# One more 2 MiB slot in the weight ring of a decoder layer with 32 experts, and the expert activation computed inside its own PSUM bank

## The chip, the cores and the metric

The kernel runs on one core of one Trainium2 chip. The metric is the device time of one execution in microseconds (us), from three timed runs. Times inside the execution come from one profiled run, whose span is the time from its first to its last instruction.

## The reference, cut to what matters

One decoder layer over 256 tokens of width 1024, all in float32. A token mixer (input projection, a spatial gate, attention, two branch products, an output product) is followed by LayerNorm and a routed FFN with 32 experts, of which every token takes 4:

```python
logits = x @ w_router + b_router                 # 256 x 32
top_val, top_idx = lax.top_k(logits, 4)
gate = softmax(top_val)
for every expert e, over the tokens that picked it:
    gu  = xe @ w_up[e] + b_up[e]                 # 1024 x 2048 weights, 8 MiB
    g   = minimum(gu[:, :F], 7.0)
    u   = clip(gu[:, F:], -7.0, 7.0)
    act = (u + 1.0) * (g * sigmoid(1.702 * g))
    y   = act @ w_down[e] + b_down[e]            # 1024 x 1024 weights, 4 MiB
out = layer_norm(alpha * h + sum of gate * y)
```

All 32 experts are used, so 32 times 12 MiB of weights are read from HBM once.

## The kernel before

**Two stages.** Stage 1 (to about 270 us of the span) is the mixer: 20 pieces of weights, split into two float32r parts and multiplied. Stage 2 is the routed FFN. In between stands the router: logits, top 4, the counts of each expert, and a sorting of the experts by their number of tokens, after which the kernel knows which expert is taken at which position p = 0 ... 31. Positions 0 and 3 always hold experts 0 and 1, so their weights can be loaded before the router has run; the other 30 expert numbers (`ids`) come out of it.

**Blocks.** A position has room for 1, 2 or 3 blocks of 32 tokens (15, 14 and 3 positions, 52 blocks in all). For each block, TensorE does `up_bias` (L696, L697: the bias rows start a PSUM bank), `up_quad` (L703: 64 instructions, four column tiles of 32 side by side), then `swiglu` runs on other engines, `act_T` transposes the activation (L720), `spread` transposes the weighted one-hot matrix (L685), `down_half` is the down product (L730: 64 instructions), `y_of` copies it out (L737) and `scatter` adds it to the output (L745). `gather` (L662) picks the tokens of a group of up to 4 blocks.

**The order on TensorE** is written out by hand (`steps`): `a` is the first half of a position's up weights, `b` the second half, `d` the down weights. The usual order is ... `b(p-1)`, `a(p)`, `d(p-1)`, `b(p)`, `a(p+1)` ..., so the bias matmuls of the next position come right after the last up product of the one before; ahead of a position with three blocks a `d` step lies in between. Small work (`act_T`, `spread`, `gather`, `scatter`) is put in between by a counter (`later`, `tick`). The order on the other engines is the framework's.

**PSUM.** The up product of a block takes one of two `mm` banks in turn (a third block of a position takes the `at` bank), all transposes share one `tp` bank. The next owner of an `mm` bank waits until `swiglu` has read it for the last time.

**`swiglu` before** (L709 to L713): VectorE clips the gate half into SBUF, ScalarE takes the sigmoid, VectorE clips the linear half into SBUF (its last read of the bank), GpSimd multiplies gate and sigmoid, VectorE forms the activation.

**The weight ring** has 10 half slots of 2 MiB, as five tiles `R0` to `R4`. Four of them are also the buffers of stage 1. `order` lists the halves in the order of loading. `free(p, k)` is called when TensorE's last product with a half has been issued; it calls `load_next`, which starts the next load into that slot on SP's DMA queue. For positions 5 to 29 (`WHOLE`) two halves are loaded with one 4 MiB DMA, when both slots of a tile are free. Ten halves can be loaded ahead of the router: both experts known beforehand, without the down weights of position 3. The eleventh load in `order` needs `ids` (L190 reads a register from it).

Of the kernel before, what the change touches and what calls it, by code (L numbers as in the profile page):

```python
# [54 lines left out]
def tile_kernel(ctx: ExitStack, tc: tile.TileContext, x, ln_in_g, ln_in_b, w_in, gmlp_ln_g, gmlp_ln_b,  # L55
# [25 lines left out]
    R = [ringp.tile([P, 8192], FT, name=f"R{i}") for i in range(4)]  # L81
# [84 lines left out]
    heads = [(0, "a"), (0, "b"), (0, "d"), (3, "a"), (3, "b")]  # L166
    order = [(p, k + h) for p, k in heads + [u for u in uses if u not in heads] for h in "01"]
# [4 lines left out]
    def half(slot):  # L172
        return R[slot // 2][:, slot % 2 * 4096:slot % 2 * 4096 + 4096]

    done = []

    def load_next(slot):
# [4 lines left out]
        n = 2 if p in WHOLE else 1  # L182
# [10 lines left out]
        if n == 2:  # L193
            assert h == 0 and slots[0] % 2 == 0 and slots[1] == slots[0] + 1
            to = R[slots[0] // 2]
        else:
            to = half(slot)
# [97 lines left out]
    def constants():  # L295
# [13 lines left out]
        k["rows"] = keep.tile([P, P], FT, name="rows_of")  # L309
        nc.gpsimd.iota(k["rows"].rearrange("p (n s) -> p n s", n=4), pattern=[[-1, 4], [0, CAP]], base=0,  # L310
                       channel_multiplier=1, **iota)
        nc.vector.tensor_scalar(rows0, k["rows"], 0.0, None, op0=OP.is_equal)
# [5 lines left out]
        k["onesf"] = keep.tile([2 * NE, P], FT, name="onesf")  # L318
# [247 lines left out]
    for i in range(n_pieces):  # L566
# [69 lines left out]
    R.append(sp2.tile([P, 8192], FT, name="R4"))  # L636
    load_next(8)
    load_next(9)
# [3 lines left out]
    low, up = 0, 64  # L642
    tables = sp2.tile([P, D + T * P], FT, name="tables")
    gT = tables[:NE + 1, :T * P].rearrange("p (t q) -> p t q", t=T)
    rkT = tables[:NE, T * P:2 * T * P].rearrange("p (t q) -> p t q", t=T)
    bd = tables[up:up + NE + 1, :D]
    gD = tables[up:up + NE + 1, D:].rearrange("p (t q) -> p t q", t=T)

    gates = sp2.tile([P, T, NE + 1], FT, name="gates")
# [24 lines left out]
    def weighted(rank, gate, k):  # L674
        ptg = sp2.tile([P, T, P], FT, name="ptg", bufs=2)
        for t in range(T):
            nc.vector.tensor_scalar(ptg[:, t].rearrange("p (n s) -> p n s", n=4),
                                    iota_s[:, None, k * CAP:(k + 1) * CAP].to_broadcast([P, 4, CAP]), rank(t), gate(t),
                                    op0=OP.is_equal, op1=OP.mult)
        return ptg  # L680

    def spread(ptg):
        ps = ps_tp()
        for t in range(T):
            nc.tensor.transpose(ps[:, t * P:(t + 1) * P], ptg[:, t], ident)  # L685
        qt = sp2.tile([P, T, P], FT, name="qt", bufs=4)
        nc.vector.tensor_copy(qt, ps[:, :T * P].rearrange("p (t q) -> p t q", t=T))
        return qt

    def bias_rows(e4):  # L690
        at = sp2.tile([P, P], FR, name="rows", bufs=2)
        nc.vector.tensor_scalar(at, const["rows"], e4, None, op0=OP.is_equal)
        return at
# [40 lines left out]

    def y_of(py):
        y = sp2.tile([P, 256], FT, name="y", bufs=3)
# [10 lines left out]


# [7 lines left out]
    keys = sp2.tile([NE, NE], FT, name="keys")  # L756
# [88 lines left out]
    def spread_row(at, j):  # L845
        ps = ps_tp()
        nc.tensor.matmul(ps, const["onesf"][at:at + 1], tables[at:at + 1, j * 512:(j + 1) * 512], start=True, stop=True)
# [3 lines left out]
    def residual(j):  # L851
        ps = spread_row(0, j)

        def part(t, todo):
            ys = []
            for i in range(2):
                y = sp2.tile([P, 256], FT, name="y", bufs=3)
                z = zn[:, t].rearrange("p (c q) -> p q c", c=NC)[:, 64 * j + 32 * i:64 * j + 32 * i + 32]
                nc.vector.scalar_tensor_tensor(y.rearrange("p (q c) -> p q c", c=NC), z, ALPHA,
                                               ps[:, i * 256:(i + 1) * 256].rearrange("p (q c) -> p q c", c=NC),  # L860
# [3 lines left out]
            def add():  # L864
                for i in range(2):
                    n = 2 * j + i
                    to = yacc[j][:, i, t * 256:(t + 1) * 256]
                    nc.tensor.matmul(to, gD[:, t], bd[:, n * 256:(n + 1) * 256], start=False, stop=False)
# [28 lines left out]
    def masks(g):  # L897
        pts[g] = sp2.tile([P, T, GRP * CAP], FT, name="pt", bufs=2)
# [110 lines left out]
    def logits(t, ps):  # L1009
# [3 lines left out]
        lt = sp2.tile([P, T, P], FT, name="ptg", bufs=2)[:, 0]  # L1013
# [3 lines left out]
    def pick(t, ps):  # L1017
        lg = sp2.tile([P, NE], FT, name="lg", bufs=2)
        nc.vector.tensor_tensor(lg, ps[:, P:P + NE], rb, op=OP.add)
        v8 = sp2.tile([P, 8], FT, name="v8", bufs=2)  # L1020
        nc.vector.max(v8, lg)
        i8 = sp2.tile([P, 8], U32, name="i8", bufs=2)
        nc.vector.max_index(i8, v8, lg)
        i4 = sp2.tile([P, TOPK], FT, name="i4", bufs=2)
        nc.vector.tensor_copy(i4, i8[:, :TOPK])
        eq = sp2.tile([P, NE, TOPK], FT, name="eq", bufs=1)
# [16 lines left out]
    nc.sync.dma_start(bd[:NE], b_down[0])  # L1043
    nc.sync.dma_start(bd[NE:], ln_mix_b)
# [17 lines left out]
    for t in range(T):  # L1062
        lg, v8 = picks[t]
        nv = sp2.tile([P, 4], FT, name="nv", bufs=2)
        nc.vector.tensor_scalar(nv[:, 0:1], v8[:, 0:1], -1.0, None, op0=OP.mult)
        ex = sp2.tile([P, NE], FT, name="ex", bufs=1)
# [13 lines left out]
    with tc.manual_schedule(engines=MS):  # L1080
        def free(p, k):
            load_next(ring[p, k])
# [14 lines left out]
        for kind, p in steps[1:-1]:  # L1097
# [3 lines left out]
            if kind == "b":  # L1101
# [8 lines left out]
                if p == LEFT_AT + 1:  # L1110
                    load_row(0, ln_mix_g)
                    load_row(32, ln_ffn_g)
                if p in RESIDUAL_AT:
                    later(1, lambda p=p: residual(RESIDUAL_AT.index(p)))
                if p == NORM_AT:
                    load_row(0, ln_ffn_b)
                if p == NE - 2:
                    gb = R[ring[p, "b0"] // 2][:, :2 * D].rearrange("p (a d) -> p a d", a=2)
# [46 lines left out]

    with tc.For_i(0, n_left) as i:
# [6 lines left out]
        ra, rbb, rd, rt = [R[ring[k] // 2] for k in ((NE - 1, "a0"), (NE - 1, "b0"), (NE - 2, "d0"), (NE - 1, "d0"))]  # L1173
        nc.sync.dma_start(ra, up_e[:, 0:8192])
        nc.sync.dma_start(rbb, up_e[:, 8192:16384])
        nc.sync.dma_start(rd.rearrange("p (h n) -> p h n", h=2), wd[bass.ds(e, 1)].rearrange("o p h n -> (o p) h n"))
        four = sp2.tile([P, 1], FT, name="four")
        nc.vector.tensor_scalar(four, cur[:, 2 * T], 4.0, None, op0=OP.mult)
        pt = sp2.tile([P, T, GRP * CAP], FT, name="pt", bufs=2)
# [54 lines left out]
```

## Time and profile before

| | |
|---|---|
| median of 3 runs | 1202.85 us (1202.83 to 1206.37) |
| profiled execution, its own time | 1203.3 us |
| its span | 1201.5 us |
| mean granted TensorE clock | 0.957 of full speed |
| busy shares: TensorE, VectorE, ScalarE, GpSimd | 92%, 35%, 18%, 9% |
| moved by DMA | 451.06 MB, 448.58 MB of it read from HBM |

The profiled execution's own time is 1.8 us longer than its span (work around the first and last instruction), and 0.45 us above the median. A DMA share of 1.00 means that all 16 DMA engines were busy for the whole stretch. TensorE's busy time counts pipelined matmuls and is no measure of a full array.

### The profile page before, as it was taken

How to read it: one execution, taken by the hardware profiler on the slowest of the kernel's cores; microseconds unless marked ns; L12 is line 12 of the kernel's file. 1: busy time of each engine (PE TensorE's matmuls, PEld its weight loads, DVE VectorE, ACT ScalarE, POOL GpSimd, SP SyncE). 2: the span in 40 equal slices, each digit the busy share in tenths (PEclk: the TensorE clock that was granted, in tenths of full speed). 3: DMA queues.
4: the chain of work that ended last, by engine and by line, in shares of the span. 5: the costliest groups of instructions: out<-in, count | busy, mean ns of one | idle time of the engine just before them, and what ended most of it. 6: DMA issues, size and time to landing. Idle time of an engine off the chain costs nothing.

```text
span 1201.5 us, 21808 instructions
## 1 busy us (share of the span) xinstructions
PE 1106.8 (92%) x9725; PEld 576.6 (48%) x9725; DVE 416.8 (35%) x779; ACT 216.2 (18%) x359; POOL 110.8 (9%) x121
## 2 busy tenths in 40 slices
PE   8999999999999889889999989999999899999794
PEld 6778788874544244343434343434333424343231
DVE  7964645554413122214132231411323223121203
ACT  5445643422201001000001010100010101010010
POOL 3800200000100000001010000000100010000000
PEclk8999999999999879889999999899999999999788
DMA  9554557667999999999999999999999999999993
GB/s 358 190 210 143 215 203 288 253 247 292 408 430 430 431 430 430 436 433 425 429 435 430 431 431 432 431 429 432 434 429 428 435 428 431 431 434 429 428 426 152
DMA packets 44208, 451.06 MB, mean 375 GB/s; under 512 B 2968, under 2 KB 3628, under 8 KB 26064
## 3 DMA queue, kind: packets, MB, share of 16 engines
q1 hardware_dynamic: 43504, 449.47, 89.3%
q8 instruction: 78, 1.28, 0.4%
q10 hardware_dynamic: 608, 0.16, 0.1%
q14 instruction: 18, 0.15, 0.0%
HBM read 448.58 MB, written 1.05 MB: 374 GB/s over the span
## 4 chain that ended last, share of the span: by engine, by line
PE 72%; DMA 21%; DVE 4%; ACT 1%; POOL 1%; issue 1%; ACTq 0%; DVEq 0%; SPq 0%; POOLq 0%
PE mm L703 20%; PE mm L530 18%; PE at L730 15%; DMA R<-in_w_down_dram 15%; DMA R<-in_w_up_dram 6%; PE tp L662 5%; PE ac L745 4%; PE tp L720 2%; PE tp L685 1%; PE mm L696 1%; POOL gg L712 1%; DVE gg L709 1%; PE at L703 1%; DVE wlo L480 1%; PE mm L697 0%
## 5 line engine op out<-in xcount | busy, mean ns | idle before, releaser
L703 PE MATMUL mm<-R,hT 128*32 128x512 f32 x3136 | 378.7, 609 | 12.7 <-DMA R<-in_w_up_dram 12.7
L730 PE MATMUL at<-R,actT 128*32 128x256 f32 x3328 | 220.4, 405 | 21.8 <-DMA R<-in_w_down_dram 14.8
L703 PEld LDWEIGHTS mm<-R,hT 128*32 128x32 f32 x3136 | 89.2, 111 | 194.1 <-issue 171.9
L709 DVE TENSOR_SCALAR gg<-mm 64x512 f32<-64x512 f32 x49 | 33.5, 683 | 360.4 <-PE mm L703 360.0
L730 PEld LDWEIGHTS at<-R,actT 128*32 128x32 f32 x3328 | 101.0, 115 | 115.2 <-issue 30.8
L712 POOL TENSOR_TENSOR gg<-gg,sg 64x512 f32<-64x512 f32 x52 | 66.4, 1277 | 837.8 <-ACT sg L710 837.8
L480 DVE TENSOR_TENSOR wlo<-R,whi 128x1024 fp32r<-128x1024 f32 x80 | 112.4, 1416 | 76.1 <-ACT whi L472 75.6
L530 PE MATMUL mm<-whi,hTh 128*128 128x512 f32 x256 | 100.6, 401 | 0.8 <-ACT R L489 0.8
L530 PE MATMUL mm<-wlo,hTh 128*128 128x512 f32 x256 | 100.0, 398 | 0.5 <-DVE wlo L480 0.5
L472 ACT ACTIVATE whi<-R 128x1024 fp32r<-128x1024 f32 x80 | 84.4, 1057 | 86.7 <-PE mm L530 81.5
L530 PE MATMUL mm<-whi,hTl 128*128 128x512 f32 x256 | 99.9, 398 | 0.0
L710 ACT ACTIVATE sg<-gg 64x512 f32<-64x512 f32 x52 | 32.8, 630 | 304.5 <-DVE gg L709 282.4
L737 ACT ACTIVATE y<-at 128x256 f32<-128x256 f32 x52 | 20.0, 384 | 333.6 <-PE at L730 333.6
L662 PEld LDWEIGHTS tp<-pt,xn 128*128 128x128 f32 x448 | 56.1, 197 | 28.7 <-DVE hT L667 17.9
L662 PE MATMUL tp<-pt,xn 128*128 128x128 f32 (+2 forms) x448 | 65.9, 291 | 0.0
L745 PE MATMUL ac<-y,qt 32*128 32x256 f32 x832 | 59.9, 402 | 0.5 <-ACT y L737 0.5
L745 PEld LDWEIGHTS ac<-y,qt 32*128 32x128 f32 x832 | 37.9, 185 | 37.8 <-issue 35.6
L670 ACT ACTIVATE hT<-tp,lm 128x128 f32<-128x128 f32 (+2 forms) x58 | 25.6, 445 | 165.8 <-PE tp L662 165.7
L530 PEld LDWEIGHTS mm<-wlo,hTh 128*128 128x128 f32 x256 | 48.0, 188 | 13.4 <-DVE wlo L480 2.3
L722 DVE COPY actT<-tp 128x256 f32<-128x256 f32 x52 | 22.1, 425 | 93.2 <-PE tp L720 93.1
L720 PEld LDWEIGHTS tp<-ident,act 64*128 64x128 f32 x208 | 28.8, 209 | 53.1 <-issue 19.5
L530 PEld LDWEIGHTS mm<-whi,hTh 128*128 128x128 f32 x256 | 48.0, 188 | 12.0 <-ACT R L489 0.9
(273 smaller groups left out, 843.7 us busy)
## 6 DMA issues: line engine op xcount, KB each, us to landing
R<-in_w_up_dram SPq DMA_DIRECT2D x50, 4096.0 KB, 34.8
R<-in_w_down_dram SPq DMA_DIRECT2D x25, 4096.0 KB, 37.2
R<-in_w_up_dram SPq DMA_DIRECT2D x28, 2048.0 KB, 12.0
R<-in_w_in_dram SPq DMA_DIRECT2D x13, 2048.0 KB, 8.7
R<-in_w_down_dram SPq DMA_DIRECT2D x13, 2048.0 KB, 33.2
R<-in_w_branch_a_dram SPq DMA_DIRECT2D x2, 2048.0 KB
R<-in_w_branch_b_dram SPq DMA_DIRECT2D x2, 2048.0 KB, 8.3
R<-in_w_out_dram SPq DMA_DIRECT2D x2, 2048.0 KB
```

The source lines that it names most:

```text
L472: nc.scalar.activation(hi, w, AF.Copy)
L480: nc.vector.tensor_tensor(lo, w, hi.bitcast(FT), op=OP.subtract)
L530: nc.tensor.matmul(ps[t], (a_l if k == 1 else a_h)[:, c, t * P:(t + 1) * P], (lo if k == 2 else hi)[:, cc], start=c == 0 and k == 0, stop= ...
L662: nc.tensor.matmul(ps[:, i * w:(i + 1) * w], zn[:, t, c * P:(c + 1) * P], pt[:, t, :w], start=t == 0, stop=t == T - 1)
L670: nc.scalar.activation(dst[:, c, :w], ps[:, i * w:(i + 1) * w], AF.Identity, scale=lm[:, 0, c:c + 1], bias=lm[:, 1, c:c + 1])
L703: nc.tensor.matmul(ps[n * CAP:(n + 1) * CAP], xs[:, c], w[:, o:o + 512], start=False, stop=c == NC - 1)
L709: nc.vector.tensor_scalar(gg, ps[:2 * CAP], LIMIT, None, op0=OP.min)
L710: nc.scalar.activation(sg, gg, AF.Sigmoid, scale=SW_ALPHA)
L712: nc.gpsimd.tensor_tensor(gg, gg, sg, op=OP.mult)
L720: nc.tensor.transpose(ps[:, c * 2 * CAP:(c + 1) * 2 * CAP], v[:, c], ident[:2 * CAP, :2 * CAP])
L730: nc.tensor.matmul(py[n * CAP:(n + 1) * CAP, :256], at[:, c, h], w[:, o:o + 256], start=h == 0 and c == 0, stop=h == 1 and c == 3)
L745: nc.tensor.matmul(to[n // 2][:, n % 2, t * 256:(t + 1) * 256], qt[s, t], y[s], start=start and t == 0, stop=stop and t == T - 1)
```

## The change

The ring gets an eleventh half slot, so the first half of position 3's down weights can also be loaded before the router. Slots 0 to 7 are now one tile, and slots 8 to 10 another. A 4 MiB load may take any two neighbouring free slots that are freed one after the other; otherwise each half is loaded by itself. Counted through the program, 75 loads of 4 MiB and 42 of 2 MiB become 61 and 70.

The room for the slot comes from smaller tables: the bias `b_down` is loaded in two halves of columns, one-hot matrices are stored once instead of four times, `onesf` is one column that is broadcast, router temporaries live in the activation buffers, and the mask buffer `pt` has one copy instead of two. Three consequences are instructions: `spread` uses eight 32-column matmuls instead of two transposes, `residual` builds its row of gains from `lm` with eight broadcast matmuls instead of loading and spreading a row, and `swiglu` works in place: sigmoid and clipped linear half are written back into the block's own PSUM bank, and VectorE does the product that GpSimd did.

```diff
-    R = [ringp.tile([P, 8192], FT, name=f"R{i}") for i in range(4)]
+    pieces = [ringp.tile([P, 8 * 4096], FT, name="R")]
+    R = [pieces[0][:, i * 8192:(i + 1) * 8192] for i in (2, 0, 1, 3)]
...
-    heads = [(0, "a"), (0, "b"), (0, "d"), (3, "a"), (3, "b")]
-    order = [(p, k + h) for p, k in heads + [u for u in uses if u not in heads] for h in "01"]
+    heads = [(0, "a"), (0, "b"), (3, "a"), (3, "b"), (0, "d")]
+    order = [(p, k + h) for p, k in heads for h in "01"] + [(3, "d0")]
+    order += [(p, k + h) for p, k in uses for h in "01" if (p, k + h) not in order]
...
-    def load_next(slot):
+    def load_next(slot, behind=None):
...
-        n = 2 if p in WHOLE else 1
+        n = 2 if p in WHOLE and k[1] == "0" and done[0] != 7 and done[0] + 1 in (done[1:] or [behind]) else 1
...
-            for slot in (4, 5, 6, 7):
+            for slot in (2, 3, 6, 7):
                 load_next(slot)
...
-            for slot in ((2, 3), (0,), (1,))[i - n_pieces + 3]:
+            for slot in ((0, 1), (4,), (5,))[i - n_pieces + 3]:
...
-    R.append(sp2.tile([P, 8192], FT, name="R4"))
-    load_next(8)
-    load_next(9)
+    pieces.append(sp2.tile([P, 3 * 4096], FT, name="R8"))
+    for slot in (9, 10, 8):
+        load_next(slot)
...
     def weighted(rank, gate, k):
-        ptg = sp2.tile([P, T, P], FT, name="ptg", bufs=2)
+        ptg = sp2.tile([P, T, CAP], FT, name="ptg", bufs=2)
...
     def spread(ptg):
         ps = ps_tp()
         for t in range(T):
-            nc.tensor.transpose(ps[:, t * P:(t + 1) * P], ptg[:, t], ident)
+            for n in range(4):
+                nc.tensor.matmul(ps[n * CAP:(n + 1) * CAP, t * P:(t + 1) * P], ptg[:, t], ident, start=True, stop=True)
...
     def swiglu(ps):
-        act = sp2.tile([2 * CAP, 512], FT, name="act", bufs=3)
-        gg = sp2.tile([2 * CAP, 512], FT, name="gg", bufs=2)
-        sg = sp2.tile([2 * CAP, 512], FT, name="sg", bufs=1)
-        nc.vector.tensor_scalar(gg, ps[:2 * CAP], LIMIT, None, op0=OP.min)
-        nc.scalar.activation(sg, gg, AF.Sigmoid, scale=SW_ALPHA)
-        nc.vector.tensor_scalar(act, ps[2 * CAP:], LIMIT, -LIMIT, op0=OP.min, op1=OP.max)
-        nc.gpsimd.tensor_tensor(gg, gg, sg, op=OP.mult)
-        nc.vector.scalar_tensor_tensor(act, act, 1.0, gg, op0=OP.add, op1=OP.mult)
-        return act
+        if not act_bufs:
+            tile_ = sp2.tile([P, 512], FT, name="act", bufs=2)
+            act_bufs.extend((tile_, o) for o in (0, 2 * CAP))
+        tile_, o = act_bufs.pop(0)
+        act = tile_[o:o + 2 * CAP]
+        gate, lin = ps[:2 * CAP], ps[2 * CAP:]
+        nc.vector.tensor_scalar(act, gate, LIMIT, None, op0=OP.min)
+        nc.scalar.activation(gate, act, AF.Sigmoid, scale=SW_ALPHA)
+        nc.vector.tensor_scalar(lin, lin, LIMIT, -LIMIT, op0=OP.min, op1=OP.max)
+        nc.vector.tensor_tensor(act, act, gate, op=OP.mult)
+        nc.vector.scalar_tensor_tensor(act, lin, 1.0, act, op0=OP.add, op1=OP.mult)
+        return act, o
...
     def residual(j):
-        ps = spread_row(0, j)
+        ps = ps_tp()
+        for c in range(NC):
+            nc.tensor.matmul(ps[:, c * 64:(c + 1) * 64], lm[:, 0, c:c + 1].to_broadcast([P, P]),
+                             ident[:, 64 * j:64 * j + 64], start=True, stop=True)
...
-        pts[g] = sp2.tile([P, T, GRP * CAP], FT, name="pt", bufs=2)
+        pts[g] = sp2.tile([P, T, GRP * CAP], FT, name="pt", bufs=1)
...
+        freed = [(p, k + h) for p, k in uses for h in "01"]
+
         def free(p, k):
-            load_next(ring[p, k])
+            i = freed.index((p, k)) + 1
+            load_next(ring[p, k], ring[freed[i]] if i < len(freed) else None)
```

## Rows read from the trace of the kernel before

**Rows 1.** The profile page, part 2: DMA rate in 40 slices of 30 us.

```profile
GB/s 358 190 210 143 215 203 288 253 247 292 408 430 430 431 430 430 436 433 425 429 435 430 431 431 432 431 429 432 434 429 428 435 428 431 431 434 429 428 426 152
```

**Rows 2.** Windows: busy us of each engine, granted clock, DMA share, GB/s.

```profile
280.00:285.00 5.00, 4.94 (x44) 2.77 (x46) 3.26 (x22) 2.10 (x4) 0.00 (x0) 1.00 0.01 2
285.00:290.00 5.00, 5.00 (x48) 2.63 (x44) 3.31 (x18) 1.45 (x4) 0.00 (x0) 1.00 0.53 184
...
763.00:1187.00 424.00, 384.13 (x4006) 164.88 (x4006) 97.12 (x218) 37.67 (x78) 29.59 (x24) 0.95 0.99 423
330.00:1170.00 840.00, 770.55 (x7814) 330.90 (x7810) 207.12 (x473) 72.79 (x149) 61.04 (x48) 0.95 1.00 431
```

**Rows 3.** Timeline of SP's queue, 267 to 291 us: start, length, DMAs issued.

```profile
267.73 0.81 SPq L212 DMA_DIRECT2D R<-in_w_up_dram  x2
...
286.49 0.38 SPq L212 DMA_DIRECT2D R<-in_w_up_dram  x1
```

**Rows 4.** What SP's queue waited for, 262 to 290 us: total, times, longest.

```profile
SPq L190 <- DVE nv L1065: 15.6, 1, 15.6
```

**Rows 5.** Loads into the ring issued from 585 to 615 us: issue to landing.

```profile
DMA to landing us min/median/max: 23.1/23.1/23.1
```

**Rows 6.** The chain that ended last, after 1100 us: start, length, what.

```profile
1161.50 24.53 DMA R<-in_w_down_dram
```

**Rows 7.** What TensorE waited for, 330 to 1187 us: total, times, longest.

```profile
PE at L730 <- DMA R<-in_w_down_dram: 14.8, 11, 2.5
PE mm L696 <- DVE act L711: 13.8, 10, 2.0
PE mm L703 <- DMA R<-in_w_up_dram: 12.7, 3, 6.1
PE tp L720 <- DVE act L713: 10.7, 3, 3.6
```

**Rows 8.** The same, 763 to 1187 us.

```profile
PE at L730 <- DMA R<-in_w_down_dram: 10.8, 9, 2.5
...
PE mm L703 <- DMA R<-in_w_up_dram: 7.8, 2, 6.1
```

**Rows 9.** Timeline of VectorE around the end of position 11 (two blocks).

```profile
602.70 0.68 DVE L709 TENSOR_SCALAR gg<-mm 64x512 f32<-64x512 f32 x1 [17.78 <-PE mm L703]
603.41 0.69 DVE L711 TENSOR_SCALAR act<-mm 64x512 f32<-64x512 f32 x1
```

**Rows 10.** Timeline of TensorE: bias matmuls of positions 12 and 13.

```profile
604.28 0.50 PE L696 MATMUL mm<-bup_h,rows 128*128 128x512 f32 x1
...
627.11 0.47 PE L696 MATMUL mm<-bup_h,rows 128*128 128x512 f32 x1 [0.96 <-DVE act L711]
```

**Rows 11.** Groups of instructions: busy us, mean ns, idle before.

```profile
L712 POOL TENSOR_TENSOR gg<-gg,sg 64x512 f32<-64x512 f32 x52 | 66.4, 1277 | 837.8 <-ACT sg L710 837.8
L710 ACT ACTIVATE sg<-gg 64x512 f32<-64x512 f32 x52 | 32.8, 630 | 304.5 <-DVE gg L709 282.4 <-POOL gg L712 22.1
L503 DVE TENSOR_TENSOR R<-mm,R 128x512 f32<-128x512 f32 x4 | 2.8, 692 | 0.0
L847 PE MATMUL tp<-tables,onesf 1*128 1x512 f32 x12 | 10.3, 952 | 2.3 <-ACT R L879 2.3
L345 PE MATMUL mm<-wr,lm 128*128 128x32 f32 x16 | 3.0, 356 | 2.4 <-DMA wr<-in_w_router_dram 2.4
```

**Rows 12.** Timeline of TensorE: transposes between up products, and the router's 32-column product.

```profile
275.29 0.65 PE L1012 MATMUL ac<-hT,wr 128*32 128x128 f32 x16
...
312.70 0.44 PE L685 MATMUL tp<-ident,ptg 128*128 128x128 f32 x2
313.07 1.06 PE L703 MATMUL mm<-R,hT 128*32 128x512 f32 x8
```

**Rows 13.** Windows after two of the four 2.0 us waits at L696.

```profile
662.00:666.00 4.00, 4.00 (x34) 1.53 (x38) 0.88 (x2) 0.00 (x0) 0.40 (x1) 1.00 1.11 479
810.00:814.00 4.00, 4.00 (x22) 1.01 (x24) 0.88 (x2) 0.00 (x0) 0.01 (x1) 0.57 1.11 475
```

More of the change, by code (lines that the diff above doesn't have):

```diff
@@ L172, in half @@
     def half(slot):
[L173 removed]
+        return pieces[slot // 8][:, slot % 8 * 4096:slot % 8 * 4096 + 4096]
     done = []
[L177 removed]
+    def load_next(slot, behind=None):
         done.append(slot)
@@ L193, in load_next @@
         if n == 2:
-            assert h == 0 and slots[0] % 2 == 0 and slots[1] == slots[0] + 1
-            to = R[slots[0] // 2]
+            lo = slots[0] % 8 * 4096
+            assert h == 0 and slots[1] == slots[0] + 1
+            to = pieces[slots[0] // 8][:, lo:lo + 8192]
         else:
@@ L307, in constants @@
         nc.gpsimd.iota(k["iota_p"], pattern=[[0, 1]], base=0, channel_multiplier=1, **iota)
[L309 to L312, printed above, removed]
+        k["rows"] = keep.tile([P, 4], FT, name="rows_of")
+        nc.gpsimd.iota(k["rows"], pattern=[[-1, 4]], base=0, channel_multiplier=1, **iota)
+        nc.vector.tensor_scalar(rows0.rearrange("p (n s) -> p n s", n=4),
+                                k["rows"][:, :, None].to_broadcast([P, 4, CAP]), 0.0, None, op0=OP.is_equal)
         k["stack"] = keep.tile([P, NE], FT, name="stack")
@@ L746, in scatter @@
                                  start=start and t == 0, stop=stop and t == T - 1)
+    y_bufs = [sp2.tile([P, 256], FT, name=f"y{i}") for i in range(2)] + [wr.rearrange("p c e -> p (c e)")]
     tab = sp2.tile([P, 2 * T + 1, NB], FT, name="tab")
@@ L755, in tile_kernel @@
     nb = sp2.tile([NE, 1], BF, name="nb")
-    keys = sp2.tile([NE, NE], FT, name="keys")
+    keys = scratch[:NE, 480:512]
     perm = sp2.tile([NE, NB], FT, name="perm")
@@ L828, in place_table @@
             if lo >= NE:
-                nc.tensor.matmul(ps[:, t * n:(t + 1) * n], const["onesf"][:NE], shift, start=False, stop=True)
+                nc.tensor.matmul(ps[:, t * n:(t + 1) * n], const["onesf"][:NE].to_broadcast([NE, P]), shift, start=False, stop=True)
             nc.tensor.matmul(ps[:, (T + t) * n:(T + t + 1) * n], gT[:NE, t], cols, start=True, stop=True)
@@ L1116, in tile_kernel @@
                     load_row(0, ln_ffn_b)
+                    load_row(32, ln_ffn_g)
                 if p == NE - 2:
-                    gb = R[ring[p, "b0"] // 2][:, :2 * D].rearrange("p (a d) -> p a d", a=2)
+                    gb = half(ring[p, "b0"])[:, :2 * D].rearrange("p (a d) -> p a d", a=2)
                     for a in range(2):
@@ L1163, in tile_kernel @@
         close()
+    kept = (ring[NE - 2, "b0"], ring[NE - 1, "a0"])
+    spare = [half(slot) for slot in range(11) if slot not in kept]
+    w_e, rt = spare[:6], spare[6]
     with tc.For_i(0, n_left) as i:
@@ L1172, in tile_kernel @@
         up_e = wu[bass.ds(e, 1)].rearrange("o p n -> (o p) n")
[L1173 to L1176, printed above, removed]
+        down_e = wd[bass.ds(e, 1)].rearrange("o p h n -> (o p) h n")
+        for h in range(4):
+            nc.sync.dma_start(w_e[h], up_e[:, h * 4096:(h + 1) * 4096])
+        for h in range(2):
+            nc.sync.dma_start(w_e[4 + h], down_e[:, h])
         four = sp2.tile([P, 1], FT, name="four")
         nc.vector.tensor_scalar(four, cur[:, 2 * T], 4.0, None, op0=OP.mult)
-        pt = sp2.tile([P, T, GRP * CAP], FT, name="pt", bufs=2)
+        pt = sp2.tile([P, T, GRP * CAP], FT, name="pt", bufs=1)
         for t in range(T):
```

80 lines of the change are left out of this document (45 added, 35 removed).

## The prediction

> **What bounds the kernel now.** I read the slices first: the DMA rate is uneven in the first ten slices, 408 GB/s in the eleventh, and then 425 to 436 until the last [rows 1]. Over 330 to 1170 us the 16 DMA engines are busy for the whole time, at 431 GB/s [rows 2]. So the second stage ends when the weights have been read; what matters is how much of them has been read before the steady stretch, and whether anything opens a hole in it.
>
> The one hole near its start is at 280 us: the share is 0.01 in one window of 5 us and 0.53 in the next [rows 2], 4.95 + 2.35 = 7.3 us without transfers. SP's queue shows why: at 267.7 us it issues the last two of the ten loads that need no `ids`, and the eleventh goes out at 286.5 us [rows 3], after 15.6 us of waiting for `ids` [rows 4]. The ring is full and the next expert is not known.
>
> Then the depth of the queue. A 4 MiB load takes 4.19 MB / 431 GB/s = 9.7 us alone. The slowest stretch for TensorE has 23.1 us from issue to landing [rows 5], so at least 13 us of other loads lie ahead of each new one, and TensorE may come that much later before the DMA engines run dry. At the end, the last quarter of the last load lands at 1161.5 + 24.5 = 1186.0 us [rows 6]; from there to the end of the span are 15.5 us of product, scatter, LayerNorm and output that the change leaves alone.
>
> TensorE is a close second. From 330 to 1187 us it waits 14.8 + 12.7 = 27.5 us for weights, 13.8 us for an `mm` bank and 10.7 us for the activation [rows 7], and its granted clock is 0.95 on average [rows 2]: 857 us times 0.05 is 43 us of full-speed work lost at the lower level.
>
> **The change part by part.**
>
> *Eleventh slot.* One more half, 2.097 MB, is loaded before `ids` is there. At 431 GB/s that is 4.9 us, and it fits into the 7.3 us hole. Order and releases of the loads that follow (experts 1 and 2) are unchanged, so the steady stretch starts as before with 2.097 MB less to read: **-4.9 us**. It can't be more by much, since the stretch has no other hole, and it is 0 if the slot is not free before 286.5 us. The slot is cut from the buffers of stage 1, whose last products end at the time of the two issues at 267.7 us [rows 3]; I take the full amount.
>
> *61 and 70 loads instead of 75 and 42.* 14 more issues on SP's queue. With 13 us or more of loads queued [rows 5] they hide; without that cover each would cost a fraction of a microsecond. 0.
>
> *`swiglu` in the bank.* Before, the bank is free when the linear half has been clipped: 602.70 to 603.41 + 0.69 = 604.10 us [rows 9], and the bias matmul of position 12 starts at 604.28 us without a wait [rows 10]. Now the bank is held to the end of the last VectorE operation: clip 0.68, sigmoid 0.63 [rows 11], product and final operation at 0.69 each (the nearest row is the product with one PSUM input, L503 [rows 11]), with about 0.15 us of hand-overs: free at about 602.70 + 2.85 = 605.55, its owner starts at 605.7 us. TensorE waits **1.4 us** where it waited 0. Behind the bias matmul in TensorE's queue stands all of the next position.
>
> How often: I went through all bias matmuls in the timeline. 13 positions follow a two-block position directly and take its first bank (604.28 is one), 0 to 1.4 us. 6 two-block positions follow a one-block position, and their second block takes its bank; there the wait of 0.96 us [rows 10] becomes 2.4. In 4 places a two-block position follows another, and the second bank was waited for 2.0 us already; that grows by about 0.4 us, because TensorE comes 1.4 us later. The 0.96 and 2.0 us waits make up the 13.8 us [rows 7]. Sum: 19 x 1.4 + 4 x 0.4 = **28 us more of TensorE**. If VectorE takes up the next block's clip in between, 0.7 us more in 17 of these places, 40 us; the lower end is 0 for those whose waits fall before data that isn't there yet.
>
> The three places where the transposes wait directly for the activation (3.6 us each [rows 7]) gain: GpSimd's 1.28 us becomes VectorE's 0.69 [rows 11], -0.6 each, **-2 us**. VectorE gets 52 x 0.69 = 36 us more over 900 us at 35% busy: hidden, but for the waits counted.
>
> *`spread`.* Two transposes take 313.07 - 312.70 = 0.37 us of TensorE's time; the same form as the new one, 16 instructions of 32 columns, takes 0.65 us with its run-out [rows 12]. Between 0 and +0.28 us; I take 0.1 since most of the difference is run-out, for 48 blocks **+5 us**, at most 13.
>
> *`residual`.* A spread row takes two instructions of 0.95 us, that overlap; eight broadcast products are 16 instructions, as in L345 with 3.0 us [rows 11]. +1 to +2 us twice: **+3 us**. Its loads fall away. `pt` with one copy, scratch in the activation buffers: masks are written after the gather of the group before has run, so I see no new wait; if there is one it is like that of a bank.
>
> **Does TensorE keep up?** More work: 28 - 2 + 5 + 3 = **34 us**. Cover: 27.5 us of waiting for weights [rows 7], which shrinks as TensorE gets later, and the share of the lost clock that follows from those waits. Half of 43 us is my choice, 21 us (some drops follow other waits). From 48 us the 4.9 us go off, by which the weights now come earlier: 43 us. 34 is less than 43. Late in the span the same sum is 9 x 1.4 + 1 + 24 x 0.1 - 1 = 15 us against 10.8 + 7.8 = 18.6 us [rows 8] plus 424 x 0.05 / 2 = 11, less 4.9: 25 us. So the end is still that of the DMA stream, by a margin of about 10 us. In between TensorE falls further behind, but the 13 us of queue [rows 5] and the new slot's 4.9 hold the DMA engines full.
>
> The forecast is made against the profiled execution: 1203.3 - 4.9 = **1198.4 us**; against the median of 1202.85, 0.45 lower, it would be 1198.0.
>
> **The rivals.**
>
> *TensorE uses up the cover (no change).* If hand-overs are longer or VectorE interleaves, the extra work is 34 + 12 to 16 us, and 3 to 7 us beyond the cover, and so much later than the shifted stream: 1201 to 1206 us. For it speaks that the margin is thin; against it that most waits fall in the middle, where waits for weights come after them.
>
> *The clock (slower).* A wait for a bank can end in the lower clock. After the four 2.0 us waits the windows show 1.00 twice and 0.57 or 0.60 twice (one of each [rows 13]); after the 0.96 us waits it stays at 1.00. At 0.57, four microseconds lose 1.7 us. If the six waits of 2.4 us and half of the 13 new ones end so, it is 12 x 1.7 = 20 us on top of 34: 54 against 43, and the end comes 11 us after the shifted stream, at 1198.4 + 11 = **1209 us**, up to 1215 with the interleaving. It decides from about 8 us beyond the cover, that is with 10 such drops. The Trainium skill, "TensorE: Matmul & The Clock Gate", section "A second HAM failure mode: psum-queue depth-cycling", describes this: PSUM banks cycled through make TensorE idle briefly between groups of matmuls so often that its clock goes up and down. By that rule all 19 waits would cost a drop; the trace agrees for half of the 2.0 us waits and for none of the 0.96 us ones.
>
> *The slot brings nothing.* If slot 8, 9 or 10 waits for a buffer of the mixer's end, its load goes out with the eleventh, and time stays at 1202 to 1204 us. Against it: the two loads of before went out right at the end of the last product [rows 3].
>
> **How the numbers follow.** About 0.3%, 3.6 us, is what a measurement of this kernel can tell from no change. Forecast 0.5 (faster), TensorE using up the cover 0.25 and a slot without effect 0.05 (same, 0.3 together), the clock 0.2 (slower). The range starts at 1196 us (the 4.9 us, and 22 / 430 of 30 us, 1.5 us, if the new slot also fills the slice with 408 GB/s [rows 1]) and reaches to the clock rival's 1209 us; above lie its worst cases, about 0.15.
>
> **What would show it.** Right: no window near 280 us with an empty DMA, a twelfth load at 286 us, 431 GB/s up to a last landing 5 us earlier, L696 waiting some 40 us in all, waits for weights cut by half or more. Wrong: the last `b` and `d` steps start well after their weights have landed, or windows under 0.95 of the clock after bank waits, or a DMA rate under 425 GB/s in the steady stretch.

## The result and the profile after

The changed kernel takes 1243.11 us (median of 4 runs, 1240.68 to 1245.65), the kernel before 1204.37 us in the same comparison: a ratio of 1.0321, with a 95% interval of 1.0306 to 1.0337. The forecast was 1198.4 us and a range up to 1209. The profiled execution took 1241.12 us, with a span of 1239.4.

The page: DMA rate in 40 slices, and the shares of the chain that ended last by engine.

```profile
GB/s 341 191 204 180 225 170 325 186 330 356 425 428 433 428 423 426 434 431 424 424 430 428 395 420 382 425 385 377 420 423 407 379 424 409 388 393 423 428 404 37
...
PE 83%; DVE 12%; ACT 3%; issue 1%; DMA 0%; ACTq 0%; POOL 0%; DVEq 0%
```

The rate is full up to the 22nd slice. In 7 of the 17 slices from there to the last but one it is below 400, where [rows 1] have 425 to 436. The chain holds no DMA: before, its last links were loads [rows 6], and now TensorE, with VectorE, sets the end.

Windows around the hole at 280 us, and of the two long stretches. The last two lines are from the end of the ramp to TensorE's last weight product, first of the changed kernel, then of the kernel before.

```profile
280.00:285.00 5.00, 4.94 (x41) 2.83 (x43) 3.26 (x21) 2.09 (x3) 0.00 (x0) 1.00 0.91 385
285.00:290.00 5.00, 5.00 (x48) 2.67 (x44) 3.38 (x21) 1.45 (x4) 0.00 (x0) 1.00 0.48 156
330.00:1170.00 840.00, 744.67 (x8174) 334.23 (x8168) 223.59 (x508) 66.81 (x142) 0.00 (x0) 0.95 0.98 414
763.00:1187.00 424.00, 376.44 (x4250) 167.88 (x4242) 116.44 (x259) 34.72 (x73) 0.00 (x0) 0.96 0.96 406
330.00:1226.00 896.00, 792.97 (x8714) 355.04 (x8708) 237.08 (x533) 72.37 (x152) 0.00 (x0) 0.95 0.96 406
```

```profile
330.00:1188.00 858.00, 784.16 (x7998) 337.37 (x7994) 210.45 (x479) 74.19 (x152) 62.30 (x49) 0.95 1.00 426
```

The first window of the hole is filled: a share of 0.91 where [rows 2] have 0.01. The second has 0.48, so about 3 us of the 7.3 are left empty. But from 330 us on TensorE needs 896 us instead of 858, 38 us more, which is the whole loss. Of these, 792.97 - 784.16 = 8.8 us are more busy time and 103.0 - 73.8 = 29.2 us more idle time. The mean clock is 0.95 in both.

SP's queue: start, length, loads issued; and its wait for `ids`.

```profile
268.00 1.28 SPq L217 DMA_DIRECT2D R<-in_w_down_dram  x3
...
286.75 10.51 SPq L217 DMA_DIRECT2D R<-in_w_up_dram  x3
...
SPq L194 <- DVE act L1096: 14.8, 1, 14.8
```

Three loads go out at 268 us where two did [rows 3]: the eleventh slot is free in time and takes its load ahead of `ids`.

What TensorE waited for, 330 to 1230 us: total, times, longest.

```profile
PE mm L712 <- DVE act L733: 67.1, 26, 3.3
PE tp L742 <- DVE act L733: 11.1, 4, 3.6
```

The wait for a bank is 67.1 us where [rows 7] have 13.8 and the prediction some 42, 54 at most. The waits for weights, 27.5 us in [rows 7], are gone from the list of this window: in it, the weights are there before TensorE.

Timelines around the end of position 11 (VectorE, ScalarE, TensorE), then one later place with a single block (VectorE, TensorE) and a `spread` behind it. In brackets: idle time before the instruction, and what ended it.

```profile
609.78 0.68 DVE L729 TENSOR_SCALAR act<-mm 64x512 f32<-64x512 f32 x1 [17.78 <-PE mm L719]
611.12 0.71 DVE L731 TENSOR_SCALAR mm<-mm 64x512 f32<-64x512 f32 x1 [0.66 <-ACT mm L730]
611.86 0.68 DVE L729 TENSOR_SCALAR act<-mm 64x512 f32<-64x512 f32 x1
612.58 0.68 DVE L732 TENSOR_TENSOR act<-act,mm 64x512 f32<-64x512 f32 x1
613.29 0.71 DVE L731 TENSOR_SCALAR mm<-mm 64x512 f32<-64x512 f32 x1
613.90 0.69 DVE L733 SCALAR_TENSOR_TENSOR act<-mm,act 64x512 f32<-64x512 f32 x1
...
610.50 0.59 ACT L730 ACTIVATE mm<-act 64x512 f32<-64x512 f32 x1 [6.64 <-DVE act L729]
...
614.74 0.77 PE L712 MATMUL mm<-bup_h,rows 128*128 128x512 f32 x1 [3.31 <-DVE act L733]
615.30 0.63 PE L713 MATMUL mm<-bup_l,rows 128*128 128x512 f32 x1
615.86 5.26 PE L719 MATMUL mm<-R,hT 128*32 128x512 f32 x24
...
639.32 0.68 DVE L729 TENSOR_SCALAR act<-mm 64x512 f32<-64x512 f32 x1 [12.70 <-PE mm L719]
...
642.12 0.69 DVE L733 SCALAR_TENSOR_TENSOR act<-mm,act 64x512 f32<-64x512 f32 x1
...
642.96 0.47 PE L712 MATMUL mm<-bup_h,rows 128*128 128x512 f32 x1 [3.05 <-DVE act L733]
643.27 0.40 PE L713 MATMUL mm<-bup_l,rows 128*128 128x512 f32 x1
643.59 4.50 PE L719 MATMUL mm<-R,hT 128*32 128x512 f32 x40
...
649.52 0.62 PE L697 MATMUL tp<-ident,ptg 128*32 128x128 f32 x16
649.96 1.04 PE L719 MATMUL mm<-R,hT 128*32 128x512 f32 x8
```

These answer to [rows 9] and [rows 10]. Three things lie in them. The clip of the linear half (L731) starts 0.66 us late, released by ScalarE's sigmoid (L730) on the other half of the same bank; before, the two clips ran back to back at 602.70 and 603.41. Then, two operations of the next block (its clip at 611.86, its second clip at 613.29) run before this block's last one. So the bank is held from 609.78 to 613.90 + 0.69 = 614.59, 4.8 us, where the prediction had 2.85: 0.66 for the sigmoid and 1.3 for the two operations of the other block are the difference. And the first matmul of the next position waits 3.31 us. Of the 26 waits, 13 are of 3.31 us and 6 of 3.05 us. In these six no second block comes in between, and the bank is held 3.5 us, as from 639.32 to 642.12 + 0.69. The last two lines give the new `spread`: 0.44 us from its start to the next product's, where [rows 12] have 0.37; the prediction added 0.1.

Windows of 4 us, one after each of these two waits.

```profile
615.74:619.74 4.00, 4.00 (x21) 0.99 (x24) 0.98 (x2) 0.00 (x0) 0.00 (x0) 0.50 0.94 406
643.96:647.96 4.00, 4.00 (x40) 1.04 (x32) 0.03 (x1) 0.00 (x0) 0.00 (x0) 1.00 0.96 410
```

After the first the granted clock is 0.50, the 1.2 GHz level, and 24 up matmuls take 5.26 us; after the second it stays at full speed and 40 of them take 4.50, which is 2.70 for 24.

### The profile page after: what moved, and what is told of

Same layout as the page of the kernel before. It is cut to its first block, busy times and chain, and to the rows that moved or that the text cites. A ratio compares the mean times of both kernels' runs of the same rounds, so it can differ in the third digit from the quotient of the medians.

```text
span 1239.4 us, 23283 instructions
## 1 busy us (share of the span) xinstructions
PE 1115.2 (90%) x10481; PEld 596.2 (48%) x10481; DVE 441.5 (36%) x831; ACT 214.3 (17%) x359; POOL 45.2 (4%) x69
## 4 chain that ended last, share of the span: by engine, by line
PE 83%; DVE 12%; ACT 3%; issue 1%; DMA 0%; ACTq 0%; POOL 0%; DVEq 0%
PE mm L719 28%; PE mm L535 17%; PE at L752 15%; PE tp L674 5%; PE ac L771 5%; PE tp L742 3%; DVE mm L731 3%; DVE act L729 3%; PE tp L697 2%; DVE act L732 2%; DVE act L733 2%; PE mm L712 1%; ACT mm L730 1%; PE at L719 1%; DVE wlo L485 1%
## 5 line engine op out<-in xcount | busy, mean ns | idle before, releaser
L719 PE MATMUL mm<-R,hT 128*32 128x512 f32 x3136 | 391.6, 627 | 0.0
L752 PE MATMUL at<-R,actT 128*32 128x256 f32 x3328 | 210.4, 392 | 7.6 <-ACT y L763 5.4
L719 PEld LDWEIGHTS mm<-R,hT 128*32 128x32 f32 x3136 | 93.7, 114 | 191.7 <-issue 183.6
L729 DVE TENSOR_SCALAR act<-mm 64x512 f32<-64x512 f32 x49 | 33.5, 683 | 335.4 <-PE mm L719 334.8
L712 PE MATMUL mm<-bup_h,rows 128*128 128x512 f32 x49 | 27.1, 553 | 67.1 <-DVE act L733 67.1
L730 ACT ACTIVATE mm<-act 64x512 f32<-64x512 f32 x49 | 29.1, 593 | 282.0 <-DVE act L729 282.0
L763 ACT ACTIVATE y<-at 128x256 f32<-128x256 f32 x34 | 13.1, 384 | 255.0 <-PE at L752 255.0
L712 PEld LDWEIGHTS mm<-bup_h,rows 128*128 128x128 f32 x49 | 10.5, 215 | 95.3 <-issue 94.9
L742 PEld LDWEIGHTS tp<-ident,act 64*128 64x128 f32 x208 | 28.8, 210 | 55.4 <-issue 29.3
L535 PEld LDWEIGHTS mm<-whi,hTl 128*128 128x128 f32 x256 | 48.0, 188 | 11.1
```

Of the source, the lines that this page charges most:

```text
L535: nc.tensor.matmul(ps[t], (a_l if k == 1 else a_h)[:, c, t * P:(t + 1) * P], (lo if k == 2 else hi)[:, cc], start=c == 0 and k == 0, stop= ...
L712: nc.tensor.matmul(ps, at, bup_h, start=True, stop=False)
L719: nc.tensor.matmul(ps[n * CAP:(n + 1) * CAP], xs[:, c], w[:, o:o + 512], start=False, stop=c == NC - 1)
L729: nc.vector.tensor_scalar(act, gate, LIMIT, None, op0=OP.min)
L730: nc.scalar.activation(gate, act, AF.Sigmoid, scale=SW_ALPHA)
L752: nc.tensor.matmul(py[n * CAP:(n + 1) * CAP, :256], at[:, c, h], w[:, o:o + 256], start=h == 0 and c == 0, stop=h == 1 and c == 3)
```

## The experiments

All are compared with the kernel before on the same chip. In e3, e4, e5 and e11 one part of the computation changes: the four buffers for activations (halves of two tiles) are reduced to two, and in the three positions with three blocks the third activation overwrites the first before it is transposed, so these kernels leave out that part of the result.

**e1: only `swiglu` in the bank**, on the kernel before (GpSimd's product goes to VectorE, sigmoid and clip into `ps`; ring, spread and all else as before).

```diff
-        nc.vector.tensor_scalar(gg, ps[:2 * CAP], LIMIT, None, op0=OP.min)
-        nc.scalar.activation(sg, gg, AF.Sigmoid, scale=SW_ALPHA)
...
+        nc.vector.tensor_scalar(act, gate, LIMIT, None, op0=OP.min)
+        nc.scalar.activation(gate, act, AF.Sigmoid, scale=SW_ALPHA)
+        nc.vector.tensor_scalar(lin, lin, LIMIT, -LIMIT, op0=OP.min, op1=OP.max)
```

> Only the activation of the change, in the kernel before: sigmoid and clipped linear half in the block's PSUM bank, product on VectorE; ring of ten slots, transposes, buffers and loads as before. If the longer hold of the bank is the whole cause, TensorE waits some 65 us at its bias matmuls (13.8 before, 67.1 after) and the time is 1240 to 1245 us. If the ring, the smaller loads, the eight-matmul spread or the single mask buffer are the cause, it stays at 1202 to 1206 us.

Measured: 1232.86 us, ratio 1.0227 (1.0201 to 1.0252). What TensorE waited for first:

```profile
PE mm L696 <- DVE act L712: 66.6, 26, 3.2
```

The same 26 waits stand here with nothing else of the change, and 28.7 of the 38.7 us come with `swiglu` alone. The time is below the 1240 to 1245 us expected if it were the whole cause; 10 us lie elsewhere (e2, e7, e14).

**e2: the changed kernel with ten slots.**

```diff
-    pieces.append(sp2.tile([P, 3 * 4096], FT, name="R8"))
+    pieces.append(sp2.tile([P, 2 * 4096], FT, name="R8"))
```

> The whole change but with ten half slots (no early half of position 3's down weights). Bank theory: TensorE sets the end, so 4.9 us of earlier weights buy nothing and their loss costs nothing: 1240 to 1246 us, as with eleven. If the slot still earns its 4.9 us under the longer waits, 1246 to 1250. If the eleventh slot with its odd split into smaller loads is the cause, well under 1240.

Measured: 1242.97 us, ratio 1.0323 (1.0305 to 1.034). The eleventh slot is worth nothing here: while TensorE waits for banks, weights that come earlier don't move the end.

**e3: sigmoid into SBUF, clip still in the bank.**

```diff
-        nc.scalar.activation(gate, act, AF.Sigmoid, scale=SW_ALPHA)
+        nc.scalar.activation(tmp, act, AF.Sigmoid, scale=SW_ALPHA)
```

> The whole change, but the sigmoid goes to SBUF instead of the PSUM bank; the clipped linear half stays in the bank, so that the bank is still held to the last operation. Theory: in the change the clip waited for the sigmoid because both write the one bank; without that VectorE runs clip and sigmoid side by side and each hold is 0.6 us shorter, the waits at the bias matmuls fall from 67 to 45 to 55 us and the time by 10 to 20 us, to 1222 to 1233. If the order of the two makes no difference, 1241 to 1245.

Measured: 1222.66 us, ratio 1.0145 (1.0098 to 1.0192). Waits of TensorE, and VectorE at the end of position 11:

```profile
PE mm L713 <- DVE act L733: 47.7, 26, 2.4
PE tp L742 <- DVE act L733: 19.1, 6, 3.5
...
608.35 0.69 DVE L729 TENSOR_SCALAR act<-mm 64x512 f32<-64x512 f32 x1 [17.78 <-PE mm L720]
609.07 0.71 DVE L731 TENSOR_SCALAR mm<-mm 64x512 f32<-64x512 f32 x1
609.81 0.69 DVE L732 TENSOR_TENSOR act<-act 64x512 f32<-64x512 f32 x1
610.53 0.68 DVE L729 TENSOR_SCALAR act<-mm 64x512 f32<-64x512 f32 x1
611.24 0.69 DVE L733 SCALAR_TENSOR_TENSOR act<-mm,act 64x512 f32<-64x512 f32 x1
```

The clip (L731) no longer waits for ScalarE, and one operation of the next block comes in between, not two: the usual wait falls from 3.31 us to between 2.00 and 2.09. The sum for the banks falls by 19.4 us, and the time by 20.5 against the changed kernel. That these two are so close is chance: the transposes (L742) wait 8.0 us longer here, and the clock loses less (39 us, against 48 in the changed kernel, summed over windows of 1 us).

**e4: both halves clipped into SBUF first**, then the final operation, the sigmoid, and the product last; the bank is read by two operations only.

```diff
+        nc.vector.tensor_scalar(tmp, gate, LIMIT, None, op0=OP.min)
+        nc.vector.tensor_scalar(act, lin, LIMIT, -LIMIT, op0=OP.min, op1=OP.max)
+        nc.vector.scalar_tensor_tensor(act, act, 1.0, tmp, op0=OP.add, op1=OP.mult)
+        nc.scalar.activation(tmp, tmp, AF.Sigmoid, scale=SW_ALPHA)
+        nc.vector.tensor_tensor(act, act, tmp, op=OP.mult)
```

> The whole change with eleven slots, without GpSimd, but gate and linear half are both clipped into SBUF first (the bank is free after two VectorE operations, as in the kernel before); final operation and sigmoid then work in SBUF in place, the product last. Bank theory: waits at the bias matmuls back at 12 to 16 us, TensorE waits for weights again, and the slot's 4.9 us show: 1196 to 1201 us. If ring, loads, spread or buffers slow the kernel, 1215 to 1245.

Measured: 1205.55 us, ratio 1.001 (1.0001 to 1.002): 0.1% above the kernel before. Waits of TensorE; then VectorE and TensorE at the end of position 11; the last link of the chain; and the window from 330 to 1170 us.

```profile
PE tp L742 <- DVE act L733: 23.6, 6, 4.2
PE at L752 <- DMA R<-in_w_down_dram: 12.9, 5, 4.1
PE mm L713 <- DVE act L730: 11.1, 10, 1.4
...
600.58 0.69 DVE L730 TENSOR_SCALAR act<-mm 64x512 f32<-64x512 f32 x1
601.46 0.50 PE L713 MATMUL mm<-bup_h,rows 128*128 128x512 f32 x1
...
1163.36 24.27 DMA R<-in_w_down_dram
...
330.00:1170.00 840.00, 766.06 (x8543) 345.58 (x8542) 234.17 (x526) 72.95 (x150) 0.00 (x0) 0.96 1.01 429
```

The bank waits are back at 11.1 us and the weights set the end again. So 37.6 us of the loss hang on how long VectorE and ScalarE keep the bank, and not on GpSimd's absence or the work of VectorE (e8 below, which does the whole computation, gives 36.9). But one thing doesn't fit: with the DMA engines at the end, the eleventh slot should show its 4.9 us (1196 to 1201 us were expected), and the last load lands at 1163.36 + 24.27 = 1187.6, 1.6 us later than before [rows 6]. The rate is 429 GB/s at a full share, not 431 [rows 2]; over 840 us that is 840 x 2 / 431 = 3.9 us. The next runs look for it.

**e5: e4 with ten slots; e6: the kernel before with `WHOLE = range(0)`**, so that each of its 75 loads of 4 MiB becomes two of 2 MiB; **e8: e4 with the sigmoid's table loaded early and the third block's activation behind the first's transposes.**

```diff
+        while len(acts) == 2:
+            pend.pop(0)[1]()
         acts[u] = swiglu(ups.pop(u))
...
+    nc.scalar.activation(scratch[:, 448:449], scratch[:, 448:449], AF.Sigmoid)
```

> The kernel of e4 (both clips first, so a bank is free after two operations), with ten ring slots instead of eleven, as before; 75 loads of 4 MiB and 42 of 2 MiB then, where e4 has 61 and 70. In e4 the DMA engines set the end again, so the slot must show here. Theory 1, a slot is worth 2.097 MB / 431 GB/s = 4.9 us: e5 = 1205.55 + 4.9 = 1210.5 us. Theory 2, the smaller loads take it back: in e4 the lead over the kernel before falls from 1.72 MB at 350 us to 0.02 MB at 1170 us with a share of 1.00 to 1.02 all the way, 1.7 MB or 4 us for 14 loads that are split; without the split e5 loses 4.9 and gains 4.0: 1206.5 us, and the DMA rate from 350 to 1150 us is 431 GB/s like before, against 429 in e4.

> The kernel before with all its weight loads of the second stage as halves of 2 MiB: its 75 loads of 4 MiB are split. Nothing else changes. Theory 2 (each split costs 0.28 us of DMA time, 4.0 us / 14): 1204.2 + 75 x 0.28 = 1225 us, the steady rate falls from 431 to about 421 GB/s at a share of 1.0. Rival (what e4 loses in the steady stretch is not the size of the loads but its own order of work): 1202 to 1206 us, 431 GB/s.

> The kernel of e4 with two mends. The table of the sigmoid is loaded on ScalarE behind the last exponential, at 287 us, by a sigmoid of one column; in e4 it loads at 302.4 us, holds up the first sigmoid by 1.28 us and with it the copies of the gather, and TensorE waits 1.46 us at 305 us, after which the DMA share falls to 0.81. And in a position of three blocks the first activation is transposed before the third is computed, so that the whole computation is done. If the ramp is what e4 lost: its lead at 330 us goes back from 1.66 to about 2.1 MB and the time falls by 1 to 1.5 us, 1204. If the small loads take the lead back at 0.28 us each, that is all there is to gain: 1204. If the erosion in the steady stretch came from the waits of TensorE instead, with full DMA engines: 1200 to 1202.

Measured: e5 1209.9 us, ratio 1.0055 (1.004 to 1.0069); e6 1205.67 us, ratio 1.0019 (1.0005 to 1.0033); e8 1206.24 us, ratio 1.0023 (1.0009 to 1.0037). The same window, one line of each kernel (e5, e6, e8):

```profile
330.00:1170.00 840.00, 766.39 (x8475) 345.74 (x8478) 233.25 (x524) 73.00 (x150) 0.00 (x0) 0.96 1.00 428
```

```profile
330.00:1170.00 840.00, 765.46 (x7818) 325.83 (x7812) 207.11 (x473) 72.57 (x149) 60.93 (x48) 0.96 1.01 429
```

```profile
330.00:1170.00 840.00, 768.66 (x8528) 349.20 (x8528) 234.11 (x526) 73.18 (x150) 0.00 (x0) 0.96 1.01 429
```

The slot is worth 1209.9 - 1205.55 = 4.4 us when the DMA engines set the end (4.9 if each is taken against the kernel before in its own comparison). The theory of the small loads falls: 75 split loads cost 2 us, so 14 cost about 0.4, and e5 has the low rate with 75 whole loads. The ramp wasn't it either: e8's time does not fall. The low rate goes with the new ring: the kernels with the old one, e1 and e7, run at the full rate in the first stretch, where all shares are full, the changed one does not (e1, e7, changed kernel, 340 to 590 us):

```profile
340.00:590.00 250.00, 219.77 (x2152) 94.59 (x2148) 71.56 (x165) 20.43 (x43) 0.00 (x0) 0.94 1.00 431
```

```profile
340.00:590.00 250.00, 218.26 (x2332) 97.70 (x2328) 70.20 (x165) 20.42 (x43) 0.00 (x0) 0.95 1.01 431
```

```profile
340.00:590.00 250.00, 219.31 (x2378) 100.53 (x2374) 71.05 (x165) 20.41 (x43) 0.00 (x0) 0.95 1.01 428
```

One thing that differs is where the ring starts. The constants ahead of it got 960 B smaller (`rows_of` and `onesf`), and its first eight slots moved from 18432 to 17472 in each partition, from a multiple of 256 B to 64 B past one. The other slots went the other way: slots 8 and 9 of the kernel before start 192 B past a multiple of 256 B, slots 8 to 10 of the changed one on a multiple.

**e9 and e12: the kernel before with its ring moved by 64 and by 128 B** by an unused tile, which moves the constants too; **e10 and e11: e8 and e5 with the ring at 17408**, a multiple of 256 B. Nothing is computed otherwise. The first diff is that of e9 (e12 has 32 for 16), the second that of e10.

```diff
+    keep.tile([P, 16], FT, name="pad")
     R = [ringp.tile([P, 8192], FT, name=f"R{i}") for i in range(4)]
```

```diff
+        three = keep.tile([NE, 3], FT, name="three")
+        k["rev_p"], k["ranked"], k["fixed"] = [three[:, i:i + 1] for i in range(3)]
...
+    sp2.tile([P, 16], FT, name="pad")
     pieces.append(sp2.tile([P, 3 * 4096], FT, name="R8"))
```

> The kernel before with an unused tile of 64 B in front of the weight ring, so that the first eight slots start at 18496 instead of 18432 in each partition (64 B past a multiple of 256 instead of on one); slots 8 and 9 move from 149696 (192 B past) to 149760 (on one). In the changed kernel and in e4, e5 and e8 the first eight slots start at 17472, 64 B past a multiple of 256, and their steady rate from 340 to 590 us is 428 to 429 GB/s at a share of 1.00 to 1.01 against 431 in the kernel before and in e1 and e7, which keep its ring. Theory 3, the start address costs this: 428.5 against 431 GB/s is 0.6% of 880 us, 5 us: 1204 + 5 = 1209 us, and 428 to 429 GB/s. Rival, another part of the change lowers the rate (the tables, the masks, the order of the slots): 1202 to 1206 us, 431 GB/s.

> The same with an unused tile of 128 B: the first eight slots start 128 B past a multiple of 256, slots 8 and 9 64 B past one. If any start off a multiple of 256 B costs the same, all ten slots pay: 1209 to 1210 us and 428 GB/s. If a multiple of 128 is enough for the eight, only slots 8 and 9 pay as before: 1204 us, 431 GB/s.

> The kernel of e8 (both clips first, eleven slots, whole computation) with three one-column constants in one tile, so that the first eight slots start at 17408 (on a multiple of 256 B); an unused tile of 64 B keeps slots 8 to 10 at 148736, which is one too. Theory 3: the steady rate goes from 428 to 431 GB/s or a little above, the lead of the eleventh slot is kept, and the time is 1206.2 - 5 = 1201 us or below, 1199 if slots 8 and 9, which are off in the kernel before, add their part. Rival (another part of the change lowers the rate): 1206 us, 428 to 429 GB/s.

> The kernel of e5 (ten slots, both clips first) with the same move of the ring to 17408. Theory 3: 1209.9 - 5 = 1205 us, level with the kernel before, whose ten slots it has, and 4.4 us above e10. Rival: 1210 us.

Measured, with the kernel before at 1204.06 us: e9 1208.47 us, ratio 1.0039 (1.0026 to 1.0052); e12 1209.22 us, ratio 1.0047 (1.0034 to 1.006); e10 1202.64 us, ratio 0.9995 (0.9979 to 1.0011); e11 1206.64 us, ratio 1.003 (1.001 to 1.005). Windows of e9, e12 and e10:

```profile
330.00:1170.00 840.00, 767.81 (x7798) 330.54 (x7795) 206.88 (x472) 73.15 (x150) 60.97 (x48) 0.95 1.00 429
```

```profile
330.00:1170.00 840.00, 768.48 (x7789) 330.27 (x7791) 206.33 (x471) 72.79 (x149) 60.97 (x48) 0.95 1.00 429
```

```profile
330.00:1170.00 840.00, 769.82 (x8547) 349.20 (x8549) 235.96 (x529) 73.17 (x150) 0.00 (x0) 0.96 1.01 430
```

An unused tile of 64 B makes the kernel before 4.4 us slower and one of 128 B 5.2 us: that the start address costs time is shown, with the rate at 429 GB/s and a share of 1.00. With the two slots that are off already before, e9 has six more slots off a multiple of 256 B and e12 eight more; an estimate from the two times is about 0.7 us for each slot in both. The way back points the same way, e10 3.6 us below e8 and e11 3.3 us below e5, but there the intervals just overlap. It doesn't return everything (1201 us or below was expected of e10, and it has 430 GB/s, not 431), and what holds the rest is open. e10 is 40 us faster than the changed kernel, but no gain over the kernel before can be told: 1.4 us at a median, with an interval around 1.

**e13: the changed kernel with its ring at 17408; e7: e1 with the new spread; e14: e2 with the old spread** (two transposes a block instead of eight small products). The diff is that of e7; e14 has the reverse.

```diff
-            nc.tensor.transpose(ps[:, t * P:(t + 1) * P], ptg[:, t], ident)
+            for n in range(4):
+                nc.tensor.matmul(ps[n * CAP:(n + 1) * CAP, t * P:(t + 1) * P], ptg[:, t], ident, start=True, stop=True)
```

> The kernel of e1 (before, with swiglu in the bank alone, 1232.86 us, TensorE sets the end) plus the new spread: eight small matmuls where two transposes stood, on 48 blocks. If the spread is what lies between e1 and the eleven- and ten-slot kernels (1242.97 for ten slots), 10 us: 1241 to 1244 us, 0.2 us a block. If it costs 0.1 us a block as the prediction took: 1237 to 1238 us. If the remainder lies elsewhere (residual, the masks with one copy, the static activation halves): 1232 to 1234 us.

> The changed kernel with its first eight slots moved from 17472 to 17408, a multiple of 256 B, by the same step as in e10. The steady rate from 340 to 590 us should go from 428 to 430 or 431 GB/s. If TensorE alone sets the end, the time stays: 1241 to 1244 us. If the start address has a part in the loss: 1238 to 1239 us.

> The changed kernel with ten slots (e2, 1242.97 us) and the spread of the kernel before: two transposes a block in place of eight small matmuls. If the spread costs the 6.5 us that e7 shows: 1236.5 us, and 3.6 us more than e1 remain for the residual, the single copy of the masks and the static halves of the activation. If it is all of the difference: 1233 us. If the waits for the bank swallow it (the spread runs in their shadow): 1241 to 1243 us.

Measured: e7 1239.37 us, ratio 1.0297 (1.0275 to 1.0319); e13 1243.88 us, ratio 1.0326 (1.0304 to 1.0347), with 429 GB/s from 340 to 590 us, where 430 or 431 were expected; e14 1240.04 us, ratio 1.0299 (1.027 to 1.0328). The address has no part in the changed kernel's own time. The spread costs 6.5 us on e1 and 2.9 us out of e2 (there the intervals overlap); that leaves 3.6 to 7.2 us for residual, masks and static activation halves, which were not told apart.

## Why the prediction was wrong

**The hole, the slot, the loads.** The slot takes its load into the hole as forecast, and its price of 4.9 us was about right: 4.4 us between e5 and e4, 4.0 between e11 and e10. That this appears in the time was wrong, because TensorE sets the end (e2: nothing).

**The step that failed is the term "`swiglu` in the bank".** Its count was right: 13 places after two-block positions and 6 behind one-block positions stand in the trace with 3.31 and 3.05 us. Its size was not: 1.4 and 2.4 were written. The prediction let the clip of the linear half run beside the sigmoid, as it did before, when the sigmoid wrote to SBUF. In the bank the two take turns, 0.66 us. And it let VectorE take up one operation of the next block in the bad case; it takes two, 1.3 us, in all 13. 13 x 3.31 + 6 x 3.05 = 61.3 us; three waits of 1.6 us that the count lacked and the four second banks of 0.25 (forecast: 2.4) make up the rest of 67.1. So the term is 67.1 - 13.8 = 53 us instead of 28, beyond its upper bound of 40. The three waits of the transposes, forecast at -2, stayed at 3.6 us each (10.7 us in all before, 11.1 now): the product takes 0.68 us on VectorE where GpSimd took 1.28, but the clip of the linear half, 0.71 us, now stands behind the sigmoid.

**The cover failed too.** It was 27.5 us of waits for weights and 21 us of lost clock. The first was used up to the last microsecond. The second never came: the mean clock is 0.95 in both kernels, because the waits for banks lower it as the waits for weights did. Summed over windows of 1 us, the clock loses 44 us of full speed before, in 13 drops, and 6 of these, with 24 us, stand at or right behind waits for weights, so that half was about the right share. In the changed kernel it loses 48 us in 17 drops, and 12 of these, with 31 us, stand at the waits for banks. So "34 is less than 43" became 53 + 0.4 us of waits and about 10 us for the small parts (e2 less e1; forecast 8) against 27.5 of cover: the sum is 36 us. The profiled loss is 38.

**The rivals.** "TensorE uses up the cover" and "the clock" named the right mechanism, a wait for a bank, with too low a price; none gave more than 1215 us. Of the 13 waits of 3.31 us, 9 are followed by a window under 0.8 of the clock, of the 6 of 3.05 us 3, and of the three of 1.6 us none: 12 drops, the number that the clock rival took. But they replace drops of before and don't come on top. The Trainium skill, "TensorE: Matmul & The Clock Gate", section "A second HAM failure mode: psum-queue depth-cycling", tells of a kernel in which frequent short idle times between groups of matmuls, as PSUM banks are cycled through, make the clock go up and down; the trace agrees for 12 of these 22 waits. The page does not say that every such wait costs a drop, as the prediction read it.

**What no step had.** The move of the ring by 960 B, a side effect of smaller constants, costs 3 to 4 us where the DMA engines set the end (e9 shows it on the kernel before; e10 and e11 point the same way), nearly what the slot brings. With the bank freed early the change is no faster than the kernel before: that is e4 and e8.

## What to carry to other kernels

Before a step is moved into a PSUM bank, write out how long the bank is then held, with every operation of each engine in its queue order, the next block's among them, and count on engines taking turns on a bank until a trace shows otherwise; then ask which matmul is queued behind it. Read the bank out with its first operations and go on in SBUF. When a tile ahead of a DMA target changes its size, look at where the target now starts.

## What the runs showed of the hardware

- VectorE's clip on partitions 64 to 127 of a bank was held until ScalarE's sigmoid on partitions 0 to 63 of it had ended. VectorE stood idle for it 29 times, 0.66 us at the end of position 11 and 19.0 us in all. The Trainium skill, "PSUM — Partial Sum Buffer", section "PSUM bank collisions raise a hardware error", says that two engines may work in different quadrants (32 partitions each) of one bank at once; this program's wait is there all the same, so it is a wait of the program as built, and whether the chip needs it was not tried.
- Where the DMA engines set the end, rings whose first eight slots start 64 or 128 B past a multiple of 256 B are filled at 428 to 429 GB/s and those with these slots on a multiple at 430 to 431 (429 where all loads are of 2 MiB, e6), all at a share of 1.00 to 1.01: a full share does not show a full rate. The Trainium skill, "DMA: Bandwidth & Descriptors", section "How a descriptor splits into AXI transactions", says that a descriptor that doesn't start on a multiple of 256 B has a first transaction that carries unused bytes; it speaks of reading, and an estimate from it would have 128 B cost twice what 64 B do. The runs show 4.4 us with eight slots off by 64 B, and 5.2 us with these off by 128 B and the other two by 64 B: they agree on the sign, not on a doubling.
- Splitting 75 loads of 4 MiB in two cost 2.0 us in all (e6), at a full share of the DMA engines.
